# Rotary embedding on one core: first unit loaded whole, last unit in halves, first store held for a landing, 16 more rows summed by VectorE

## The chip, the cores and the metric

The kernel runs on one core of a Trainium2 chip. The time is the device time of one execution, in microseconds (us). Before the change the median of five runs is 85.15 us (85.01 to 85.94). The profile is that of one execution, which took 85.06 us.

The engines are TensorE (PE in the profile; PEld is its weight loads), VectorE (DVE), ScalarE (ACT), GpSimd (POOL) and SyncE (SP), which only issues transfers here. Sixteen DMA engines move the data.

## The reference

The input x is 8 x 8 x 1024 x 64 in fp32, 16.8 MB, and the two tables are 1024 x 32. Each row of 64 is split into halves and rotated:

```python
x_first, x_second = x[..., :half], x[..., half:]
out_first  = x_first * cos_cached - x_second * sin_cached
out_second = x_first * sin_cached + x_second * cos_cached
```

So an output element takes two products and one sum, and every byte of x is read once and every byte of the result is written once.

## The kernel before, in words

**Units and chunks.** The 65536 rows are cut into 8 units of 8192 rows. A unit lies in SBUF as 128 partitions of 64 rows, 4096 fp32 a partition, 2 MB. All 8 units have their own place (lines 60 to 72), so no load waits for room. Unit 0 is worked on first, with the tables still in PSUM; units 1, 3, 4, 5, 6, 7 are cut into chunks of 24, 24 and 16 rows (unit 7: 24, 16 and 24), and of unit 2 only rows 40 to 64 go this way. That makes 19 chunks, numbered 0 to 18: chunks 0 to 2 are unit 1, 3 is unit 2's, 4 to 6 unit 3, 7 to 9 unit 4, 10 to 12 unit 5, 13 to 15 unit 6, 16 to 18 unit 7.

**Tables.** TensorE spreads sine and cosine over the partitions (L221), ScalarE copies them to SBUF (L229, `keep`), and VectorE multiplies unit 0 by them straight from PSUM in four pieces (`first`, 8, 16, 16 and 16 rows); the first 8 rows of unit 0 are done by POOL alone (`on_pool`).

**A chunk.** ScalarE copies its rows from SBUF to one of two PSUM buffers (L119, `stage`; even and odd chunks take turns). VectorE makes all four products of the chunk in one instruction (L112, `products`). The sums of the products are made by three engines: TensorE adds 16 rows at a time as matmuls with the identity and its negative into one PSUM accumulator (L171, L172, `pe_sums`), ScalarE copies that back to SBUF (L177, `pe_back`), and POOL does the other rows in two instructions, a subtraction and an addition (L115, L116, `pool_sums`). The tables `on_pe`, `back` and `behind` say after which chunk each of these is put into its engine's program. The chunks named in `whole` are done by VectorE alone: two multiplications and two sums (`alone`). Before the change that is only chunk 18, unit 7's rows 40 to 64.

**Order.** The order on each engine is the order of the program; an engine works through its own list and waits where its inputs are missing. After the products of chunk c the loop (lines 250 to 263) has ScalarE stage chunk c + 2, then copy back, TensorE sum, POOL sum and SP store, as the tables say. So a staging copy can stand behind a copy back on ScalarE, and the next matmuls wait until the accumulator has been copied back.

**Transfers.** SP issues, in this order: the sine table, unit 0 in two halves (L82), units 1 to 7 (L84), three small loads of one row (L89), and the stores (L149). The cosine table goes through ScalarE's queue. The issues share eight completion semaphores in turn, so that an issue also waits until the transfer eight issues earlier has landed: unit 7's load for unit 0's first half, the first row load for its second half. Stores wait for the sums they write out. The first store also waits for the staging copy of chunk 9 (`gate`, lines 255 to 257 and `first_store`), though it does not use its data; stores 1, 2, ... stand behind it on SP.

Of the kernel before, what the change touches and what calls it, by code (L numbers as in the profile page):

```python
# [8 lines left out]
def kernel(  # L9
# [7 lines left out]
    nc = tc.nc  # L17
    fp32 = mybir.dt.float32
    TT = mybir.AluOpType
    P = nc.NUM_PARTITIONS  # L20

    b, h, seq, hd = x.shape
    half = hd // 2
    R = 64
    F = R * hd
    T = R * half
    n_u = (b * h * seq) // (R * P)
# [8 lines left out]
    xf = x.rearrange("b h s d -> (b h s d)").rearrange(  # L36
        "(u p m) -> u p m", p=P, m=F)
# [16 lines left out]
    xt, sv, px = {}, {}, {}  # L54
# [21 lines left out]
    for eng, i, t in ((nc.sync, 0, sin_cached), (nc.scalar, 1, cos_cached)):  # L76
        eng.dma_start(out=raw[:, i * BK // 2:(i + 1) * BK // 2],
                      in_=t.rearrange("(q n) j -> q (n j)", q=P))


    for m0, m1 in ((0, F // 2), (F // 2, F)):
        nc.sync.dma_start(out=xt[0][:, m0:m1], in_=xf[0][:, m0:m1])  # L82
    for u in range(1, n_u):
        nc.sync.dma_start(out=xt[u], in_=xf[u])  # L84


    row = const.tile([1, 3 * hd], fp32, name="row")
    for i in range(3):
# [9 lines left out]
        out=sel.rearrange("q (k r j) -> q k r j", k=N, j=S),  # L98
        in_=plus.rearrange("q (j k) -> q k j", k=N).unsqueeze(2).to_broadcast([P, N, N, S]))
# [9 lines left out]
        return t[:, n0:n1].unsqueeze(2).to_broadcast([P, n1 - n0, 2, half])  # L109

    def mul(eng, o, a, t):
        return eng.tensor_tensor(out=o, in0=a, in1=t, op=TT.mult)  # L112

    def sums(eng, o, c, s):
        eng.tensor_tensor(out=o[:, :, 0], in0=c[:, :, 0], in1=s[:, :, 1], op=TT.subtract)  # L115
        eng.tensor_tensor(out=o[:, :, 1], in0=c[:, :, 1], in1=s[:, :, 0], op=TT.add)  # L116

    def stage(pt, u, n0, n1):
        return nc.scalar.copy(out=pt[:, :(n1 - n0) * hd], in_=xt[u][:, n0 * hd:n1 * hd])  # L119

    def products(xr, u, n0, n1, t):


        n = n1 - n0
        m = K if u == 2 else 0
        mul(nc.vector, px[u][:, n0 - m:n1 - m].rearrange("p n t (k j) -> p n t k j", k=2),
            xr.rearrange("p (n o f) -> p n o f", o=1, f=hd).to_broadcast([P, n, 2, hd])
            .rearrange("p n t (k j) -> p n t k j", k=2),
            t.unsqueeze(3).to_broadcast([P, n, 2, 2, half]))

    def alone(pt, u, n0, n1):
        s = sv[4] if u == 7 else sv[u]
        xr, sr, pr = rows(xt[u], n0, n1), rows(s, n0, n1), rows(pt, 0, n1 - n0)
        mul(nc.vector, sr, pr, tab(sn, n0, n1))
        mul(nc.vector, pr, pr, tab(cs, n0, n1))
        sums(nc.vector, xr, pr, sr)
# [22 lines left out]
    st, acc, q = {}, {}, []  # L159
# [6 lines left out]
    def pe_sums(u, n0):  # L166
        acc[u, n0] = q[2].tile([P, 2 * BK], fp32, name="acc")
        a = acc[u, n0].rearrange("p (k n j) -> p k n j", k=2, j=half)
        xr, sr = rows(xt[u], n0, n0 + G), rows(sv[u], n0, n0 + G)
        for k in range(2):  # L170
            nc.tensor.matmul(a[:, k], plus, xr[:, :, k], start=True, stop=False)  # L171
            nc.tensor.matmul(a[:, k], plus if k else minus, sr[:, :, 1 - k],  # L172
                             start=False, stop=True)

    def pe_back(u, n0):
        a = acc[u, n0].rearrange("p (k n j) -> p n k j", k=2, j=half)
        nc.scalar.copy(out=rows(xt[u], n0, n0 + G), in_=a)  # L177
# [3 lines left out]
    last = ((0, 24), (24, 40), (40, 64))  # L181
    chunks = [(u, n0, n1) for u in (1, 3, 4, 5, 6, 7) for n0, n1 in (last if u == 7 else cuts)]
    chunks.insert(3, (2, K, R))
    whole = {(7, 40)}
    on_pe = {0: (1, 0), 4: (3, 0), 6: (3, 16), 7: (4, 0), 9: (4, 16), 11: (5, 0),
             13: (6, 0), 14: (6, 16)}
    back = {2: (1, 0), 6: (3, 0), 7: (3, 16), 9: (4, 0), 11: (4, 16), 12: (5, 0),
# [5 lines left out]
        7: [(first_store,), (store, 1), (store, 2), (store, 3)],  # L193
        9: [(pool_sums, 4, 32, 64)],
        11: [(store, 4)],
        12: [(pool_sums, 5, 16, 64), (store, 5)],
        15: [(pool_sums, 6, 32, 64)],
        16: [(store, 6), (pool_sums, 7, 0, 24)],
        17: [(store, 7, 0, 24), (pool_sums, 7, 24, 40), (store, 7, 24, 40)],
# [3 lines left out]
    def put(c):  # L203
        if c < len(chunks):
            u, n0, n1 = chunks[c]
            st[c] = q[c % 2].tile([P, 3 * BK], fp32, name="st")
            return stage(st[c], u, n0, n1)

# [29 lines left out]
    one.close()  # L240
    q.append(pool(ctx, "q0", "right"))
    put(0)
    first(6, 2)
    keep(6, 2)
    pool_sums(0, H, R)
    two.close()
    q += [pool(ctx, "q1", "left"), pool(ctx, "q2", "left")]
    put(1)
    on_pool(2, 0, K // 2)
    for c, (u, n0, n1) in enumerate(chunks):  # L250
        if (u, n0) in whole:
            alone(st[c], u, n0, n1)
        else:
            products(st[c][:, :(n1 - n0) * hd], u, n0, n1, tb4[:, n0:n1])
        staged = put(c + 2)
        if c == 7:
            gate = staged
        if c in back:
            pe_back(*back[c])
        if c in on_pe:  # L260
            pe_sums(*on_pe[c])
        for f, *args in behind.get(c, ()):
            f(*args)
# [29 lines left out]
```

## Time and profile before

| | |
|---|---|
| median of five runs | 85.15 us (85.01 to 85.94) |
| profiled execution | 85.06 us, span 83.3 us |
| busy: VectorE, POOL | 66.7 us, 67.3 us |
| busy: PE, ScalarE | 46.5 us, 37.9 us |
| HBM read, written | 17.04 MB, 16.78 MB, 406 GB/s over the span |
| SP's queue, share of 16 DMA engines | 96.1% |

The span is the time from the first to the last instruction; the profiled execution's time has another 1.76 us around it. Times inside the profile count from the start of the span. The line numbers (L112) are those of the kernel before. In the rows of a timeline the columns are start, duration, engine, line, operation, what it writes and reads with shapes, and in brackets the idle time of the engine before it and what ended that. DMA transfers of a stretch are counted by their start, so the share of a short stretch can be above 1 or dip without a pause.

### The profile page before, as it was taken

Reading aid. Unit: us, or ns where it says so; the run is one execution under the profiler, and the core shown is the slowest. Engines: PE = TensorE matmul, PEld = TensorE weight load, DVE = VectorE, ACT = ScalarE, POOL = GpSimd, SP = SyncE. Lnnn points to the kernel's source line nnn. Section 1 sums busy time; section 2 is a strip of 40 time slices with the busy share of each in tenths; the row PEclk is TensorE's granted clock in tenths of the full one; section 3 lists DMA queues with packets and bytes.
Section 4 is the critical chain, followed back from the end, with each engine's and each line's share of the span. In section 5 each row is a group of like instructions: output and inputs, shape, how many; then the busy total and the mean of one; then the engine's idle time right before and its main releaser. Section 6 shows DMA issues by size and latency. Waiting matters only on the chain.

```text
span 83.3 us, 385 instructions
## 1 busy us (share of the span) xinstructions
PE 46.5 (56%) x82; PEld 17.9 (22%) x82; DVE 66.7 (80%) x27; ACT 37.9 (46%) x34; POOL 67.3 (81%) x38
## 2 busy tenths in 40 slices
PE   3899991005994007970977949369959495000000
PEld 2234430003430004410413324034233140000000
DVE  3104699899999999999999999999949999991000
ACT  4320244994069534269429680890095767000000
POOL 3007969699999999999999999999999999992000
PEclk9999999975559755699999999985899999955555
DMA  1999999999999999999999999999999999999992
GB/s 16 342 417 449 460 417 417 441 417 464 409 441 433 394 464 409 456 417 401 456 410 393 401 472 393 449 433 386 480 401 433 441 386 488 394 409 402 408 422 121
DMA packets 3030, 33.82 MB, mean 406 GB/s; under 512 B 342, under 2 KB 598, under 8 KB 982
## 3 DMA queue, kind: packets, MB, share of 16 engines
q1 hardware_dynamic: 2886, 33.69, 96.1%
q10 hardware_dynamic: 144, 0.13, 0.5%
HBM read 17.04 MB, written 16.78 MB: 406 GB/s over the span
## 4 chain that ended last, share of the span: by engine, by line
POOL 58%; issue 9%; DVE 7%; PE 7%; DMA 3%; ACT 3%; POOLq 2%
POOL w L116 23%; POOL w L115 21%; POOL w L112 14%; DVE w L112 7%; PE tab L221 7%; DMA w<-in_cos_cached_dram 3%; ACT st L119 3%; POOLq L288 2%; ACT tb L229 0%; POOLq L115 0%
## 5 line engine op out<-in xcount | busy, mean ns | idle before, releaser
L112 DVE TENSOR_TENSOR w<-st,tb 128x3072 f32<-128x3072 f32 (+2 forms) x19 | 54.2, 2929 | 1.4 <-ACT st L119 1.4
L171 PE MATMUL acc<-w,plus 128*128 128x512 f32 x32 | 20.6, 732 | 21.7 <-ACT w L177 8.9
L119 ACT COPY st<-w 128x1536 f32<-128x1536 f32 (+1 forms) x19 | 24.8, 1310 | 13.9 <-DVE w L112 13.9
L115 POOL TENSOR_TENSOR w<-w 128x1024 f32<-128x1024 f32 (+4 forms) x12 | 26.2, 2186 | 1.8 <-DVE w L112 1.7
L116 POOL TENSOR_TENSOR w<-w 128x1024 f32<-128x1024 f32 (+4 forms) x12 | 26.2, 2184 | 0.0
L112 POOL TENSOR_TENSOR w<-w,tb 128x1280 f32<-128x1280 f32 (+1 forms) x6 | 14.2, 2360 | 5.7 <-DMA w<-in_x_dram 5.5
L171 PEld LDWEIGHTS acc<-w,plus 128*128 128x128 f32 x32 | 6.6, 227 | 33.6 <-issue 19.8
L112 DVE TENSOR_TENSOR w<-w,tab 128x2048 f32<-128x2048 f32 (+1 forms) x4 | 7.9, 2018 | 5.7 <-PE tab L221 5.7
L177 ACT COPY w<-acc 128x1024 f32<-128x1024 f32 x8 | 8.1, 1010 | 8.9 <-PE acc L172 8.9
L172 PE MATMUL acc<-w,minus 128*128 128x512 f32 x16 | 10.7, 757 | 0.0
L221 PE MATMUL tab<-w 128*128 128x512 f32 x16 | 9.1, 732 | 0.2 <-DMA w<-in_cos_cached_dram 0.2
L229 ACT COPY tb<-tab 128x1024 f32<-128x1024 f32 (+1 forms) x5 | 4.2, 843 | 8.9 <-DVE w L112 6.0
L172 PE MATMUL acc<-w,plus 128*128 128x512 f32 x16 | 8.2, 592 | 0.0
L221 PEld LDWEIGHTS tab<-w 128*128 128x128 f32 x16 | 3.7, 242 | 6.3 <-issue 6.3
L172 PEld LDWEIGHTS acc<-w,minus 128*128 128x128 f32 x16 | 3.8, 239 | 5.2 <-issue 5.2
L172 PEld LDWEIGHTS acc<-w,plus 128*128 128x128 f32 x16 | 3.3, 206 | 4.5 <-issue 4.5
L216 PE MATMUL tab<-plus 128*128 128x512 f32 x2 | 2.1, 1138 | 1.4 <-POOL plus L95 1.4
L97 DVE COPY w<-plus 128x1024 f32<-128x1024 f32 x1 | 1.1, 1087 | 1.3 <-POOL plus L95 1.3
L100 ACT ACT_TABLE_LOAD x1 | 1.3, 1283 | 1.1 <-PEq L277 1.1
L112 DVE TENSOR_TENSOR st<-st,tb 128x1536 f32<-128x1536 f32 x1 | 1.8, 1757 | 0.0
L115 DVE TENSOR_TENSOR w<-st,w 128x768 f32<-128x768 f32 x1 | 1.0, 958 | 0.0
L116 DVE TENSOR_TENSOR w<-st,w 128x768 f32<-128x768 f32 x1 | 0.9, 947 | 0.0
(10 smaller groups left out, 3.2 us busy)
## 6 DMA issues: line engine op xcount, KB each, us to landing
w<-in_x_dram SPq DMA_DIRECT2D x7, 2048.0 KB, 29.2
out_dram<-w SPq DMA_DIRECT2D x7, 2048.0 KB, 9.2
w<-in_x_dram SPq DMA_DIRECT2D x2, 1024.0 KB, 5.5
out_dram<-w SPq DMA_DIRECT2D x2, 768.0 KB, 6.5
out_dram<-w SPq DMA_DIRECT2D x1, 512.0 KB, 5.0
w<-in_cos_cached_dram ACTq DMA_DIRECT2D x1, 128.0 KB, 2.8
w<-in_sin_cached_dram SPq DMA_DIRECT2D x1, 128.0 KB, 2.6
row<-in_x_dram SPq DMA_DIRECT2D x3, 0.2 KB
```

The source lines that it names most:

```text
L100: nc.scalar.mul(out=minus, in_=plus, mul=-1.0)
L112: return eng.tensor_tensor(out=o, in0=a, in1=t, op=TT.mult)
L115: eng.tensor_tensor(out=o[:, :, 0], in0=c[:, :, 0], in1=s[:, :, 1], op=TT.subtract)
L116: eng.tensor_tensor(out=o[:, :, 1], in0=c[:, :, 1], in1=s[:, :, 0], op=TT.add)
L119: return nc.scalar.copy(out=pt[:, :(n1 - n0) * hd], in_=xt[u][:, n0 * hd:n1 * hd])
L171: nc.tensor.matmul(a[:, k], plus, xr[:, :, k], start=True, stop=False)
L172: nc.tensor.matmul(a[:, k], plus if k else minus, sr[:, :, 1 - k], start=False, stop=True)
L177: nc.scalar.copy(out=rows(xt[u], n0, n0 + G), in_=a)
L216: nc.tensor.matmul(tp[6][:, :BK], plus, plus.unsqueeze(1).to_broadcast([P, BK // P, P]), start=True, stop=True)
L221: nc.tensor.matmul(t[:, k * BK:(k + 1) * BK], sel[:, (b + k) * P:(b + k + 1) * P], rt, start=True, stop=True)
L229: nc.scalar.copy(out=tb[:, b * BK:(b + n) * BK], in_=tp[b])
L288: with _tile.TileContext(nc) as tc:
```

## The change

Unit 0 is loaded in one transfer instead of two, and unit 7 in two halves instead of one. The first store's extra wait is for the landing of unit 7's first half instead of the staging copy of chunk 9. Chunk 12 (unit 5, rows 48 to 64) goes from the products instruction to `alone`, so that VectorE also makes its sums, and POOL's sums of unit 5 end at row 48. The functions `mul` and `stage` return nothing now, which changes no instruction.

```diff
-    for m0, m1 in ((0, F // 2), (F // 2, F)):
-        nc.sync.dma_start(out=xt[0][:, m0:m1], in_=xf[0][:, m0:m1])
-    for u in range(1, n_u):
-        nc.sync.dma_start(out=xt[u], in_=xf[u])
+    def load(u, m0, m1):
+        return nc.sync.dma_start(out=xt[u][:, m0:m1], in_=xf[u][:, m0:m1])
+
+    for u in range(n_u - 1):
+        load(u, 0, F)
+    gate = load(7, 0, F // 2)
+    load(7, F // 2, F)
...
-    whole = {(7, 40)}
+    whole = {(5, 48), (7, 40)}
...
-        12: [(pool_sums, 5, 16, 64), (store, 5)],
+        12: [(pool_sums, 5, 16, 48), (store, 5)],
...
-        staged = put(c + 2)
-        if c == 7:
-            gate = staged
+        put(c + 2)
```

`alone` for unit 5 multiplies the staged rows by sine into SBUF and by cosine in PSUM, and then makes the two sums from the one and the other, 16 rows in each of its four instructions.

More of the change, by code (lines that the diff above doesn't have):

```diff
@@ L111, in mul @@
     def mul(eng, o, a, t):
-        return eng.tensor_tensor(out=o, in0=a, in1=t, op=TT.mult)
+        eng.tensor_tensor(out=o, in0=a, in1=t, op=TT.mult)
     def sums(eng, o, c, s):
@@ L118, in stage @@
     def stage(pt, u, n0, n1):
-        return nc.scalar.copy(out=pt[:, :(n1 - n0) * hd], in_=xt[u][:, n0 * hd:n1 * hd])
+        nc.scalar.copy(out=pt[:, :(n1 - n0) * hd], in_=xt[u][:, n0 * hd:n1 * hd])
     def products(xr, u, n0, n1, t):
@@ L206, in put @@
             st[c] = q[c % 2].tile([P, 3 * BK], fp32, name="st")
-            return stage(st[c], u, n0, n1)
+            stage(st[c], u, n0, n1)
     one, two = ExitStack(), ctx.enter_context(ExitStack())
```

## The prediction

> **What bounds the kernel now.** I read the engines by slice first, then DMA traffic in chosen stretches, then SP's timeline, and only then the chain that ended last.
>
> From the page's slices, and from the table of stretches (columns: from:to, length, granted TensorE clock, share of the 16 DMA engines, GB/s):
>
> ```profile
> PEclk9999999975559755699999999985899999955555
> DMA  1999999999999999999999999999999999999992
> ```
> ```profile
> 4.00:9.00 5.00, 1.00 1.02 426
> 9.00:42.00 33.00, 0.79 1.00 429
> 42.00:43.00 1.00, 1.00 0.94 394
> 43.00:72.00 29.00, 0.94 1.01 429
> 73.00:82.00 9.00, 0.50 0.99 408
> ```
>
> From 4 to 82 us the DMA engines are never free. All loads and stores go through SP's one queue, so the span is start-up, plus 33.6 MB of x and result at about 429 GB/s (78 us), plus a landing. The page's chain names POOL for 58%, but POOL only matters where its result comes too late to keep that queue filled. So the question is where the queue is nearly empty. SP's timeline shows when each transfer is issued:
>
> ```profile
> 6.66 0.33 SPq L84 DMA_DIRECT2D w<-in_x_dram  x1
> 9.14 0.29 SPq L89 DMA_DIRECT2D row<-in_x_dram  x1
> 41.45 0.38 SPq L149 DMA_DIRECT2D out_dram<-w  x1
> 64.96 0.33 SPq L149 DMA_DIRECT2D out_dram<-w  x1
> 70.93 0.33 SPq L149 DMA_DIRECT2D out_dram<-w  x1
> ```
>
> The last three are stores 0, 5 and 6. The DMA view gives times to landing: unit 7's load lands at 6.66+36.7 = 43.36, store 0 at 41.45+6.8 = 48.25, store 2 at 48.96+9.0 = 57.96, store 3 at 53.59+9.2 = 62.79, store 4 at 58.18+9.4 = 67.58: one unit every 4.85. So store 5 lands near 72.4, and the last store lands at 75.94+6.5 = 82.44. How early must a store be issued? At the change from loads to stores, the stretches show engines that had run dry starting again together, 0.90 to 1.05 after the issue at 41.45:
>
> ```profile
> 42.05:42.35 0.30, 1.00 0.67 273
> 42.35:42.50 0.15, 1.00 2.33 983
> ```
>
> Landing is seen some 0.35 after the last data (nothing starts after 82.1, the landing is at 82.44). So store 5's data end at 72.05, and store 6, issued at 70.93, can move from 71.83 to 71.98. **Store 6's issue has 0.1 us to spare (0 to 0.3).** Store 5 has 67.58-0.35-1.05-64.96 = 1.2; stores 1 to 4 and the three of unit 7 have 1 us or more.
>
> What sets store 6? ScalarE's timeline: the last copy back of TensorE's sums (L177) ends at 70.86. It is the end of a relay on one PSUM accumulator: unit 5's eight matmuls 54.81 to 60.20, copy, unit 6's first eight 61.31 to 65.0, copy, its second eight 66.11 to 69.8, copy.
>
> ```profile
> 60.24 1.01 ACT L177 COPY w<-acc 128x1024 f32<-128x1024 f32 x1 [4.14 <-PE acc L172]
> 65.05 1.01 ACT L177 COPY w<-acc 128x1024 f32<-128x1024 f32 x1 [1.50 <-PE acc L172]
> 69.85 1.01 ACT L177 COPY w<-acc 128x1024 f32<-128x1024 f32 x1 [0.61 <-PE acc L172]
> ```
>
> The relay is started by VectorE: chunk 11's products end at 52.34, ScalarE stages the next chunk and copies back (53.75 to 54.76), and the matmuls begin at 54.81.
>
> **Part 1, unit 0 whole.** VectorE's and POOL's first pieces need now the whole 2 MB instead of 1 MB. The halves' landings show in SP's own waits: unit 7's load was issued at 6.66, when half 0 had landed; the first row load at 9.14, when half 1 had. The bytes ahead are the same, so the whole lands at about 9.1 (it can't be before half 0's 6.66 nor after unit 1's load, seen in the second row load's issue at 14.04; half 1's 9.14 is the nearest row by far).
>
> ```profile
> 7.43 1.22 DVE L112 TENSOR_TENSOR w<-w,tab 128x1024 f32<-128x1024 f32 x1 [5.01 <-PE tab L221]
> 9.34 2.29 DVE L112 TENSOR_TENSOR w<-w,tab 128x2048 f32<-128x2048 f32 x1 [0.69 <-PE tab L221]
> ```
>
> Before: 7.43, then 9.34 (waiting for tables), 11.54, 13.74. After: 9.2, and with no more table waits 10.34 (+1.14, a start-to-start of 0.08 less than 1.22), 12.54, 14.74. The third piece ends at 14.82 instead of 13.82; table copy and staging on ScalarE follow it, and chunk 0 starts at 17.25 instead of 16.25. **VectorE is late by 1.0.** It has no idle from there to 61.07, so nothing wins this back. POOL: its four pieces take 4.10, 9.2 to 13.3; the next two, 3.57, to 16.9; then it waits for VectorE's fourth piece (17.0, was 16.0): late by 1.0 too, and busy from there on. One load fewer to issue at the start moves no data earlier.
>
> [...]
>
> **Part 2, unit 7 in halves, and the gate.** Eight unit loads plus one cut remain nine issues. The half lands 1 MB, 2.45 us, before 43.36: 40.9. Store 0 is then issued at about 41.0 instead of 41.45, where it waited for ScalarE's staging copy (ends 41.38). Behind it on SP wait all other stores; store 1 follows in 0.5, the others wait for their sums anyway. The 0.06 share missing in 42 to 43 may vanish: 0 to 0.06 us, on engines that had finished early. The last engines, which end unit 7's load near 43, did not stop there, so I take 0. The second half's issue waits for unit 0's landing (9.1), 30 us before its turn. Cost: none.
>
> **Part 3, VectorE sums 16 rows of unit 5.** Chunk 12's product (2.28, start-to-start 2.20) becomes two multiplications of 1024 and two sums of 512. The rows for 1536 and 768:
>
> ```profile
> 69.88 1.75 DVE L112 TENSOR_TENSOR w<-st,tb 128x1536 f32<-128x1536 f32 x1
> 71.54 1.76 DVE L112 TENSOR_TENSOR st<-st,tb 128x1536 f32<-128x1536 f32 x1
> 73.33 0.96 DVE L115 TENSOR_TENSOR w<-st,w 128x768 f32<-128x768 f32 x1
> 74.21 0.95 DVE L116 TENSOR_TENSOR w<-st,w 128x768 f32<-128x768 f32 x1
> ```
>
> 1024 elements last 1.22 (row of 7.43), 512 by the slope (1.04 ns each) 0.69; start to start 1.14+1.25+0.61+0.61 = 3.61, **+1.41** (1.2 to 1.6). These rows ran beside a busy POOL, so no stretching is added. Part of it is covered, since VectorE waited later:
>
> ```profile
> 62.21 2.29 DVE L112 TENSOR_TENSOR w<-st,tb 128x2048 f32<-128x2048 f32 x1 [1.14 <-ACT st L119]
> ```
>
> With both delays chunk 12 runs 53.26 to 56.87, 13 to 60.14, 14 to 63.41. Chunk 15's staging copy, behind the copy back of unit 5's sums (60.24+1.0), ends at 63.2, so VectorE no longer waits: chunk 15 starts at 63.41, late by 1.2 only. POOL loses a third of unit 5's sums (3.47 and 3.49 for 48 rows, 2.33 and 2.32 start to start for 32): unit 5 ends at 59.07+4.65 = 63.7 instead of 64.9, store 5 is issued 1.2 earlier, and that buys nothing, as store 4's data run until 67.2. POOL then waits for chunk 15 (65.7), ends unit 6 at 70.4, unit 7's at 73.9 and 76.4: 1 us late, with 3 us to spare in the queue.
>
> **Sum.** The relay is shifted by chunk 11's 1.0; chunk 12's extra lies beside unit 5's 5.4 us of matmuls. Staging copies do not stand in its way (chunk 17's 66.96 to 67.98, chunk 18's 69.0 to 70.44, copy back from 70.85). Store 6 is issued at 71.93, its data move from 72.98 at the latest instead of 72.05 to 72.12: **+0.87**. Behind it stand 4 MB already waiting, so the end moves as much: 85.06+0.87 = 85.9. The profiled 85.06 is its span 83.3 and 1.76 around it; the median of five is 85.15, so I quote the same number against it.
>
> **How the clock enters.** Unit 5's matmuls took 5.40 at a mean clock of 0.68; the next eight took 3.7 at 1.00. Were unit 5's at 1.00, before would not change (the queue is full), and after would be held by VectorE instead: chunk 16 ends at 68.95, staging 1.44, copy 1.0, store 6 at 71.4: +0.35, 85.4. Were unit 6's at half clock as well, up to +1.7 more: 87.6. [...]
>
> **Rivals.**
> - *Not slower: the whole load lands early.* Place: VectorE's first piece. If unit 0 lands at 8.2 or earlier, the third piece still starts at 11.54 and the relay is not late; store 6 goes out by 71.05 and the time stays at 85.0 to 85.2. For it: only the first slices are below full rate. Against it: 9.14. It decides below a shift of 0.15.
> - *The relay or the start is worse than the rows.* A second half-clock stretch, a later landing, or a chunk 12 longer than its rows: each 0.1 on the relay costs 0.1, since no spare is left; 86.1 to 87.6.
> - *The gate doesn't open at the half.* If the halves land together (43.36), store 0 goes out at 43.5, its data start at 44.5, and the queue is dry 1.6: 86.7. Against it: unit 0's halves landed 2.5 apart.
>
> **How the numbers follow.** Likeliest, store 6 late by 0.35 to 0.87: 0.55, of which the profile's own clock gives the point, 85.9. Worse relay or start: 0.25. Early landing, no change: 0.12. Gate: 0.04. Faster, if the start runs at the full rate (from 2 to 4 us it moved 343 GB/s, 0.4 us short of 429): 0.04, worth up to 0.4. The range, 85.1 to 86.8, takes in the first, the third in part, the gate and half of the second. About 1% is what a measurement of this kernel can tell from no change: 84.3 to 86.0. Slower than that: the second and the gate, and a quarter of the first, 0.42; faster 0.03; same 0.55.
>
> **What would show it.** First VectorE piece at 9.2; chunk 0 at 17.25; store 0 issued near 41.0; store 5 near 63.75, store 6 near 71.9; a dip of the DMA share near 72.5 where there was none; VectorE's 1.14 gone. A first piece at 8, or store 6 by 71.05, would make the prediction wrong, as would a dry queue anywhere else.

## The result, and the profile after

The changed kernel takes 85.61 us in the median of 43 executions (85.12 to 86.85), the kernel before 85.03 (80 executions). The ratio is 1.0058, with a 95% interval of 1.0045 to 1.0070: **slower by 0.5 us**, less than the 1% by which the prediction tells a change from none. Executions more than 1.5% above the fastest of their kernel are left out of the ratio and of the counts below.

The median hides two groups. Sorted by the mean TensorE clock that was granted, and with the profiled execution among them, 21 executions at 0.843 to 0.867 took 85.12 to 85.35 (median 85.22), and 20 at 0.814 to 0.833 took 85.59 to 86.24 (median 85.72). Nothing lies between. Within the second group six are at 0.832 or 0.833 (85.59 to 85.75) and fourteen at 0.814 to 0.820 (85.62 to 86.24, median 85.85); none of the fourteen has a profile.

The profiled execution is one of the first group: 85.16, span 83.4. Its slices on the page, TensorE's granted clock and the share of the DMA engines:

```profile
PEclk9999999955589985559999999999999999655555
DMA  1999999999999999999999999999999999799993
```

There is no low clock between 37 and 71 us now, where the profile before had one, and one slice of the DMA row, near 71 us, falls to 7 in the middle of the stores; before, all were 9 there. The table of stretches puts a number on it (from:to, length, clock, DMA share, GB/s). The row for 71 to 72 of the kernel before stands first; its share from 71 to 73 was 0.93:

```profile
71.00:72.00 1.00, 1.00 1.10 459
```
```profile
43.00:71.00 28.00, 1.00 1.01 431
71.00:72.00 1.00, 0.75 0.31 131
71.00:73.00 2.00, 0.62 0.77 328
```

SP's timeline, with stores 0, 5 and 6:

```profile
40.91 0.38 SPq L152 DMA_DIRECT2D out_dram<-w  x1
63.59 0.33 SPq L152 DMA_DIRECT2D out_dram<-w  x1
71.20 0.33 SPq L152 DMA_DIRECT2D out_dram<-w  x1
```

Store 0 goes out 0.54 earlier than before, store 5 1.37 earlier, and store 6 0.27 later; its data begin only after 72.0. VectorE's timeline shows both delays, the first piece (8.99, was 7.43), chunk 0 (17.03, was 16.25) and the four instructions of chunk 12:

```profile
8.99 1.22 DVE L115 TENSOR_TENSOR w<-w,tab 128x1024 f32<-128x1024 f32 x1 [6.56 <-DMA w<-in_x_dram]
17.03 3.36 DVE L115 TENSOR_TENSOR w<-st,tb 128x3072 f32<-128x3072 f32 x1 [0.23 <-ACT st L122]
53.04 1.22 DVE L115 TENSOR_TENSOR w<-st,tb 128x1024 f32<-128x1024 f32 x1
54.17 1.22 DVE L115 TENSOR_TENSOR st<-st,tb 128x1024 f32<-128x1024 f32 x1
55.43 0.69 DVE L118 TENSOR_TENSOR w<-st,w 128x512 f32<-128x512 f32 x1
56.03 0.68 DVE L119 TENSOR_TENSOR w<-st,w 128x512 f32<-128x512 f32 x1
```

And ScalarE's timeline shows what held store 6 in this execution. The copy back (L180) does not wait for TensorE here; it stands behind chunk 18's staging copy (L122), and that waited 2.16 for VectorE's chunk 16, whose products must be done before chunk 18 may take its buffer:

```profile
68.74 1.44 ACT L122 COPY st<-w 128x1536 f32<-128x1536 f32 x1 [2.16 <-DVE w L115]
70.12 1.01 ACT L180 COPY w<-acc 128x1024 f32<-128x1024 f32 x1
```

### The profile page after: what moved, and what is told of

The parts are those of the page before. It is cut to its first block, busy times and chain, and to the rows that moved or that the text cites. A ratio compares the mean times of both kernels' runs of the same rounds, so it can differ in the third digit from the quotient of the medians.

```text
span 83.4 us, 391 instructions
## 1 busy us (share of the span) xinstructions
PE 44.2 (53%) x82; PEld 17.2 (21%) x82; DVE 67.9 (81%) x30; ACT 37.9 (46%) x34; POOL 65.1 (78%) x38
## 4 chain that ended last, share of the span: by engine, by line
DVE 36%; POOL 20%; issue 10%; DMA 9%; ACT 8%; PE 4%; POOLq 2%; SPq 0%; DVEq 0%
DVE w L115 36%; POOL w L118 12%; DMA w<-in_x_dram 9%; POOL w L119 8%; ACT st L122 7%; PE acc L174 2%; POOLq L289 2%; PE acc L175 2%; ACT w L180 1%; SPq L77 0%; DVEq L115 0%; ACT tb L232 0%; POOLq L118 0%
## 5 line engine op out<-in xcount | busy, mean ns | idle before, releaser
L115 DVE TENSOR_TENSOR w<-st,tb 128x3072 f32<-128x3072 f32 (+3 forms) x19 | 53.2, 2871 | 0.2 <-ACT st L122 0.2
L122 ACT COPY st<-w 128x1536 f32<-128x1536 f32 (+1 forms) x19 | 24.9, 1310 | 18.5 <-DVE w L115 17.2
L174 PE MATMUL acc<-w,plus 128*128 128x512 f32 x32 | 19.7, 701 | 23.6 <-ACT w L180 8.6
L118 POOL TENSOR_TENSOR w<-w 128x1024 f32<-128x1024 f32 (+4 forms) x12 | 24.9, 2077 | 2.3 <-DVE w L115 2.2
L119 POOL TENSOR_TENSOR w<-w 128x1024 f32<-128x1024 f32 (+4 forms) x12 | 25.0, 2082 | 0.0
L180 ACT COPY w<-acc 128x1024 f32<-128x1024 f32 x8 | 8.1, 1008 | 3.8 <-PE acc L175 3.8
L175 PE MATMUL acc<-w,minus 128*128 128x512 f32 x16 | 9.8, 696 | 0.0
L224 PE MATMUL tab<-w 128*128 128x512 f32 x16 | 8.5, 695 | 0.3 <-DMA w<-in_cos_cached_dram 0.3
L175 PE MATMUL acc<-w,plus 128*128 128x512 f32 x16 | 8.2, 592 | 0.0
L115 DVE TENSOR_TENSOR st<-st,tb 128x1024 f32<-128x1024 f32 (+1 forms) x2 | 3.0, 1490 | 0.0
L118 DVE TENSOR_TENSOR w<-st,w 128x512 f32<-128x512 f32 (+1 forms) x2 | 1.6, 824 | 0.1
L119 DVE TENSOR_TENSOR w<-st,w 128x512 f32<-128x512 f32 (+1 forms) x2 | 1.6, 814 | 0.0
```

The source lines that it names most:

```text
L224: nc.tensor.matmul(t[:, k * BK:(k + 1) * BK], sel[:, (b + k) * P:(b + k + 1) * P], rt, start=True, stop=True)
```

## The experiments

**The second group.** The changed kernel was profiled twice more.

> The changed kernel once more, for a trace of the other group. Theory: if its mean clock is 0.833 or less, unit 5's or unit 6's matmuls took about 5.4 instead of 3.7 in it, store 6 is issued at 71.7 to 72.2 and the time is 85.6 to 86.2; if it is 0.843 or more, it repeats the profile (71.2, 85.2). Rival: with the low clock store 6 is issued at 71.2 as well.

The first of these repeated the profile: clock 0.850, 85.17, store 6 issued at 71.21.

> As the look before it: with a mean clock of 0.833 or less store 6 at 71.7 to 72.2 and 85.6 to 86.2, else 71.2 and 85.2.

The second had a mean clock of 0.832 and took 85.82, span 84.0. Its clock row, and its stretches for unit 5's matmuls and unit 6's two groups (columns: length, PE busy, clock, DMA share, GB/s):

```profile
PEclk9999999985559995557999999975999999855555
```
```profile
55.60:61.10 5.50, 5.40 (x8) 0.69 1.00 429
62.10:65.90 3.80, 3.70 (x8) 1.00 0.99 423
67.00:70.70 3.70, 3.69 (x8) 1.00 0.99 425
```

Unit 5's eight matmuls took 5.40, against 3.70 in the profile of the first group:

```profile
55.50:59.30 3.80, 3.70 (x8) 1.00 1.02 435
```

With the low clock ScalarE's last copy back waits for TensorE, and store 6 follows:

```profile
70.72 1.01 ACT L180 COPY w<-acc 128x1024 f32<-128x1024 f32 x1 [0.45 <-PE acc L175]
```
```profile
71.81 0.33 SPq L152 DMA_DIRECT2D out_dram<-w  x1
```

So these two executions are the two cases of the prediction: the relay through TensorE's accumulator holds store 6 (71.81) where unit 5's matmuls had the low clock (0.69), VectorE holds it (71.20) where they had not (1.00). The DMA share from 71 to 73 is 0.43 here. The rival falls, since store 6 does move with the clock. That the fourteen executions at 0.814 to 0.820 are of the same kind is taken from their times and was not traced.

**One part at a time.** First unit 0 whole in the kernel before, nothing else.

```diff
-    for m0, m1 in ((0, F // 2), (F // 2, F)):
-        nc.sync.dma_start(out=xt[0][:, m0:m1], in_=xf[0][:, m0:m1])
-    for u in range(1, n_u):
+    for u in range(n_u):
         nc.sync.dma_start(out=xt[u], in_=xf[u])
```

> The kernel before with unit 0 loaded whole and nothing else changed. Theory (queue and relay): VectorE starts at 9.0 instead of 7.4 and chunk 0 at 17.0, 0.8 late; the first store still waits for chunk 9's staging copy, so it is issued at 42.2 instead of 41.45, and the DMA engines run dry by about 0.5 at the change from loads to stores; what comes later is then covered by that delay. 85.3 to 85.6, ratio 1.003 to 1.007, no second dip at store 6. Rival (the late start costs nothing, the 16 rows do): 85.0, ratio 1.000.

Measured: 86.11, ratio 1.0149 (1.0121 to 1.0178), more than the whole change costs. The staging copy of chunk 9, on which store 0 still waits, began only at 41.23, store 0 to 42.33 (before: 41.45), and the stretches at the change from loads to stores, in the profiled execution of 86.17, show the engines at rest for most of a microsecond:

```profile
41.00:42.00 1.00, 1.00 1.16 492
42.00:43.00 1.00, 1.00 0.09 34
43.00:44.00 1.00, 1.00 1.25 524
```

The place was as expected, and the queue did not run dry at store 6 (issued at 70.46). The size was not: the engines stood still for some 0.9 us instead of 0.5 (the share missing from 42 to 43), the span grew by 0.8 (83.3 to 84.1), and 0.3 more lies outside the span (2.07 instead of 1.76). Where that 0.3 comes from was not followed.

Then the 16 rows alone: the two lines of `whole` and `behind` in the kernel before.

> The kernel before with VectorE summing unit 5's rows 48 to 64 and nothing else changed. Theory: the relay to store 6 begins with chunk 11, ahead of the new work, so store 6 is issued by 71.0, store 5 at 63.8 instead of 64.96, and the queue stays full: ratio 1.000 (0.998 to 1.002). Rival (VectorE's 1.4 us more are the cost): VectorE's chunks 13 to 18 are 0.3 to 1.4 late, store 6 with them, ratio 1.004 or more.

Measured: 85.02, ratio 1.0013 (0.9991 to 1.0035). The profiled execution of this kernel had a mean clock of 0.832 (before: 0.833), and store 6 was issued at 70.87 (before: 70.93). Store 5 went out at 62.77, not 63.8: the expected figure has POOL 1 us late, which comes of unit 0 whole and isn't so here. VectorE's 1.4 us are free on their own, and the rival falls.

The changed kernel with unit 5's sums on POOL again:

> The changed kernel with POOL summing unit 5 to row 64 as before; unit 0 whole, unit 7 in halves and the gate at its first half stay. Theory: store 0 is issued at 40.9 and no engine stops there; at a full TensorE clock store 6 is issued near 70.4, in time, and the time is at or a little under the kernel before (84.8 to 85.1); where unit 5's matmuls get half the clock store 6 comes at 71.7 and the time is 85.5 to 85.7. Ratio 0.998 to 1.003. Rival (unit 0 whole is the cost by itself): ratio 1.005 as in the changed kernel.

Measured: ratio 1.0047 (1.0015 to 1.0078), a miss: it is the ratio that the rival named, and half of the few executions had a low clock. The clocks tell more than the ratio: five at 0.849 to 0.854 took 84.84 to 85.37 (four of them under 85), four at 0.816 or 0.817 took 85.67 to 85.83; one at 0.824 took 84.81, so a low mean clock alone does not make an execution long. In the profiled one, at 0.853, store 6 went out at 70.27 and no slice was dry. So with unit 5's matmuls at the full clock unit 0 whole costs nothing once the gate no longer hangs on the staging copy, and most of the 0.9 between this 70.27 and the changed kernel's 71.20 comes of the 16 rows, which are not free there (unit 0 landed 0.1 earlier in this execution). At the low clock it costs 0.8 without the 16 rows too, as the rival says; that is from the times of the four, none of which has a profile.

The changed kernel with unit 0 in halves again:

```diff
-    for u in range(n_u - 1):
+    load(0, 0, F // 2)
+    load(0, F // 2, F)
+    for u in range(1, n_u - 1):
         load(u, 0, F)
```

> The changed kernel with unit 0 loaded in halves as before; the gate at unit 7's first half and the 16 rows summed by VectorE stay. Theory: VectorE starts at 7.4 again, store 6 goes out by 71.0 whatever the clock, the queue is full from the first load to the last store: ratio 1.000 (0.998 to 1.002). Rival (gate or 16 rows cost): ratio 1.003 or more.

Measured: 85.18, ratio 1.0036 (1.0020 to 1.0052), a miss, and where the rival said. Store 6 was issued at 69.39 and the profile shows no dry queue. Its spans are 0.1 to 0.2 longer than those of before and the time outside the span 0.1 longer (1.91, with 1.78 in the runs of before beside it). It has one transfer more than either kernel; whether that is the reason stays open. That the gate and the 16 rows aren't what costs in the changed kernel, once store 6 is in time, is seen in the first group of the next kernel, which has both.

**What holds store 6 at the full clock.** In the changed kernel the last copy back was put ahead of chunk 18's staging copy.

```diff
+        if c == 16:
+            pe_back(*back[c])
         put(c + 2)
-        if c in back:
+        if c in back and c != 16:
             pe_back(*back[c])
```

> The changed kernel with ScalarE's last copy back (unit 6, rows 16 to 32) ahead of chunk 18's staging copy instead of behind it. Theory (at the full clock it is chunk 16 and the staging copy of chunk 18 that hold store 6): in executions with the full clock store 6 is issued at 70.2 to 70.5 instead of 71.2 and the time falls to 84.8 to 85.0; with unit 5's matmuls at half the clock nothing is gained, 85.6 to 86.1. Rival (store 6 is not what costs at the full clock): the lower group stays at 85.1 to 85.35.

Measured: ratio 1.0031 (1.0001 to 1.0060); seven executions at 0.846 to 0.854 took 84.66 to 85.10, three at 0.812 to 0.819 took 85.69 to 85.85. ScalarE's timeline of the profiled one (84.84), and SP's:

```profile
69.55 1.01 ACT L180 COPY w<-acc 128x1024 f32<-128x1024 f32 x1 [2.87 <-PE acc L175]
70.45 1.45 ACT L122 COPY st<-w 128x1536 f32<-128x1536 f32 x1
```
```profile
70.63 0.33 SPq L152 DMA_DIRECT2D out_dram<-w  x1
```

The slower group's time is unchanged, the faster one's falls by about 0.3 and lies where the kernel before is. That is the expectation, give or take 0.1 (85.0 and 70.5 were its upper ends), and the rival falls: at the full clock the staging copy behind chunk 16 was the cost.

**The pause ahead of unit 5's matmuls.** Next, `c == 16` was made `c in (11, 16)`, so that ScalarE also frees the accumulator for unit 5 before it stages chunk 13.

> The changed kernel with two of ScalarE's copies back put ahead of the staging copy they stood behind: unit 4's rows 16 to 32 (ahead of chunk 13's) and unit 6's rows 16 to 32 (ahead of chunk 18's). Theory: TensorE's idle time ahead of unit 5's matmuls falls from 1.97 to 1.1 like its other pauses, so it keeps the full clock there and the executions with a mean clock of 0.81 to 0.833 disappear; the relay starts 0.9 earlier, store 6 is issued by 70.7 in all, one group of times at 84.7 to 85.1, ratio 0.997 to 1.001. Rival (the low clock has nothing to do with that pause): two groups of clocks stay, the upper times nearer, 85.0 to 85.5.

Measured: 85.13, ratio 1.0015 (0.9993 to 1.0037). TensorE's pause ahead of unit 5 fell as meant, from

```profile
55.59 0.70 PE L174 MATMUL acc<-w,plus 128*128 128x512 f32 x1 [1.97 <-ACT w L180]
```

in the changed kernel to

```profile
54.58 0.70 PE L174 MATMUL acc<-w,plus 128*128 128x512 f32 x1 [1.10 <-ACT w L180]
```

and nine executions, all at a clock of 0.845 or more, took 84.75 to 85.46, four of them above the 85.1 of the expectation. The other three took 86.34, 86.42 and 87.81 at 0.813, 0.850 and 0.834. So the low-clock group near 85.7 is gone, but on few executions, and it isn't shown that the low clock never comes. The edit also did not remove the pause but moved it. TensorE now stands still 1.96 ahead of unit 6's second group, and in this execution the eight matmuls behind it ran at the full clock (1.00 from 66 to 71):

```profile
65.57 0.70 PE L174 MATMUL acc<-w,plus 128*128 128x512 f32 x1 [1.96 <-ACT w L180]
```

That the pause lowers the clock is therefore not shown: with the same 1.97 ahead of them, unit 5's matmuls took 5.40 at 0.68 in the profile of before and 5.40 at 0.69 in that of the changed kernel at 0.832, but 3.70 at 1.00 in that of the changed kernel's first group. This kernel is no faster than the one before, which has the same full queue.

**Failed as meant, useful otherwise.** Three extra matmuls into an unused PSUM bank were to keep TensorE busy through that pause, in the changed kernel and in the one with unit 5's sums on POOL.

```diff
         put(c + 2)
+        if c == 10:
+            for _ in range(3):
+                nc.tensor.matmul(st[12][:, 2 * BK:], plus,
+                                 plus.unsqueeze(1).to_broadcast([P, BK // P, P]),
+                                 start=True, stop=True)
```

> The changed kernel with three more matmuls of the identity into an unused PSUM bank of chunk 12's staging buffer, placed between unit 4's last matmuls and unit 5's, so that TensorE's 2 us of idleness there shrinks to 0.7. Theory (the granted clock of the relay makes the two groups of times): all executions stay at 85.1 to 85.4 with a mean clock of 0.845 or more, ratio 1.002 to 1.004. Rival (the spread comes from the transfers): half of the executions stay at 85.6 to 86.2, ratio 1.006.

> The changed kernel with POOL's sums of unit 5 to row 64 as before and the three more matmuls ahead of unit 5's. Theory: store 6 is issued near 70.3 in every execution, the queue never runs dry, 84.8 to 85.0 throughout, ratio 0.997 to 1.001. Rival: the upper group (85.67 to 85.83 without the more matmuls) stays, ratio 1.004.

Measured: 89.9 (ratio 1.0537) and 87.67 (1.0306). The bank belongs to chunk 12's staging buffer, and VectorE's chunk 12 was made to wait for the matmuls:

```profile
56.32 1.23 DVE L115 TENSOR_TENSOR w<-st,tb 128x1024 f32<-128x1024 f32 x1 [3.18 <-PE st L261]
```

So they do not test what the times would be without the pause. Store 6 came at 76.00 and 73.09 in the two, which serves below.

The last one, in the kernel before, makes the matmul calls of unit 6's rows 16 to 32 twice, eight instead of four, to lengthen the relay:

```diff
-        for k in range(2):
+        for k in ((0, 0, 1, 1) if (u, n0) == (6, 16) else (0, 1)):
             nc.tensor.matmul(a[:, k], plus, xr[:, :, k], start=True, stop=False)
```

> The kernel before with four of unit 6's last eight matmuls made twice, 1.7 us more on the relay to store 6, the same result. Theory (store 6 has 0.1 to spare where unit 5's matmuls ran at half the clock and 1.5 where they did not): up to 1.6 more in the first kind of execution (86.5), 0.1 to 0.3 in the second; store 6 is issued 1.7 later and a dip of the DMA share stands before its data. Rival (the time follows POOL's or VectorE's last sums, not store 6): ratio 1.000.

Measured: ratio 1.0274 (1.0232 to 1.0316), far above the expectation. The added work was mis-sized: each call is two matmuls in the trace, so the relay grew by eight matmuls (sixteen instead of eight in the trace), 3.4 us, not 1.7. In the profiled execution, at 0.859, store 6 was issued at 71.91; without the 3.4 it would have been 68.5, so 2.5 was spare and 0.9 was not: three executions at 0.853 to 0.861 have spans of 83.9 to 84.1, 0.8 more than before, and one at 0.836 has 86.0, 2.8 more. Their time outside the span is 1.8 to 3.45, which was not explained, so only the spans are used.

**All profiles together.** Issue of store 6, and the span, both in the same execution:

| kernel | store 6 issued | span | difference |
|---|---|---|---|
| unit 0 in halves | 69.39 | 83.3 | 13.9 |
| no 16 rows | 70.27 | 83.2 | 12.9 |
| two copies back first | 70.39 | 83.1 | 12.7 |
| one copy back first | 70.63 | 83.1 | 12.5 |
| 16 rows alone | 70.87 | 83.3 | 12.4 |
| before | 70.93 | 83.3 | 12.4 |
| changed | 71.20 | 83.4 | 12.2 |
| changed, once more | 71.21 | 83.4 | 12.2 |
| changed, low clock | 71.81 | 84.0 | 12.2 |
| longer relay | 71.91 | 84.1 | 12.2 |
| no 16 rows, more matmuls | 73.09 | 85.3 | 12.2 |
| changed, more matmuls | 76.00 | 88.2 | 12.2 |

Up to about 71.0 the issue does not matter, and the span is 83.1 to 83.3 whatever it is. From 71.2 on the span is the issue plus 12.2, over 4.8 us of range and in four kernels. (The kernel with unit 0 whole alone is not in the table, since it ran dry at store 0.)

## Why the prediction was right or wrong, point by point

- **What bounds it: right.** The queue is the limit and store 6 is its one weak place; the table shows the corner between 70.93 and 71.20, where the prediction put it (70.93 and 0.1 to spare).
- **Part 1: right in place, a little too dear.** VectorE's first piece came at 8.99, not 9.2, and chunk 0 0.78 late, not 1.0. The load landed by 8.91 (the issue of unit 7's second half waits for it): the term "half 1's 9.14" stood for a landing 0.2 too late. That is within what executions differ by: the same wait for half 1 ended at 8.92 with the 16 rows alone and at 9.06 with the longer relay.
- **Part 2: right against the kernel before, and half understood.** Store 0 went out at 40.91 (41.0 was said) and no gain from it is seen; the gate was not run alone. But "Cost: none" left out what the step does for part 1. Without it, part 1 takes store 0's gate along, and unit 0 whole alone costs 1.2 us, more than the whole change.
- **Part 3: right in its price, and free only on its own.** Chunk 12 took 3.6 (53.04 to 56.63 when chunk 13 may start); VectorE's 1.14 of idle time is gone; store 5 at 63.59 bought nothing. Alone it is free (1.0013). On top of unit 0 whole, with unit 5's matmuls at the full clock, it moves store 6 from 70.27 to 71.20: VectorE's delays add up there. The prediction has this only in its case of the full clock.
- **The sum: right in both cases, each 0.1 to 0.2 high.** For the low clock the prediction said store 6 at 71.93 and 85.9: 71.81 and 85.82 in the trace, 85.72 in the median of that group. For the full clock it said 71.4 and 85.4: 71.20, and 85.22 in the median. Both misses go with part 1: chunk 0 began 0.12 and 0.22 earlier than the 17.25 of the prediction in these two traces, store 6 0.12 and 0.2 earlier.
- **The choice of the point: the step that cost accuracy.** 85.9 was the case of the profiled clock. The measured median, 85.61, is at the lower edge of the second group (85.59 to 86.24), because the two groups are nearly equal in number; had two of the second fallen into the first it would have been 85.35, so how near the point came is in part luck. The same program gives both groups; no run here shows what puts an execution in the one or the other.
- **Rivals.** Early landing did not occur (8.9, not 8.2). The gate did open at the half. The profiles need no worse relay; the fourteen executions at 0.814 to 0.820 have no profile, and one of them, 86.24, lies where the prediction put a worse relay (86.1 to 87.6).

## What to carry to other kernels

Where one transfer queue is full from start to end, as here, look for the time not in the busiest engine but in the spare of each store: the end of the data of the store ahead, less its own issue, less the time from issue to data. Find the store with the least, follow what releases it back through the engines, and price every edit at that one place; an edit that does not reach it is free, as the 16 rows were alone, and an edit that is free alone can reach it together with another, as the same rows did on top of unit 0 whole. If that chain passes through TensorE and the traces show two clocks on it (here the same eight matmuls took 5.40 at 0.69 and 3.70 at 1.00), price it at both before choosing one number.

## What the runs showed of the hardware that was not expected

- TensorE's clock behind a pause, for the groups of eight matmuls after the first 17 us. In the profile of before, pauses of 6.97, 5.83, 2.55, 1.10, 1.10, 1.97, 1.10 and 1.10 us stood ahead of the eight groups, which ran at mean clocks of 0.60, 0.69, 1.00, 1.00, 1.00, 0.68, 1.00 and 1.00. In the changed kernel's, at 85.16, the pauses were 8.22, 6.73, 1.74, 1.10, 1.10, 1.97, 1.10 and 1.62, the clocks 0.70, 0.60 and then 1.00 six times. With the 0.69 behind 1.97 in the changed kernel at 85.82, the same 1.97 us in the same program went either way (5.40 us and 3.70 for eight matmuls). What decides between them was not found.
- Store data began 0.8 to 1.0 us after the issue in the changed kernel, with the engines at rest late in the stores: store 6 was issued at 71.20, the DMA share was 0.01 from 71.5 to 72.0, and the data started from 72.0 to 72.2. The prediction, from store 0 of the kernel before, took 0.90 to 1.05.
- The time outside the span is not the same for all kernels: 1.8 for most, 1.9 to 2.0 with one transfer more and also with three matmuls more, 2.0 to 2.1 with unit 0 whole alone, and up to 3.45 with eight matmuls more. No cause was found.
